# A Hymba layer on one core: other banks in the output projection, token sums kept in DRAM, buffers laid out anew

## The chip, the core and the metric

The kernel runs on one core of a Trainium2 chip. TensorE (PE in the profile) multiplies matrices into PSUM banks, VectorE (DVE) and ScalarE (ACT) work element by element, GpSimd (POOL) and SyncE (SP) issue the transfers between DRAM and the core's on-chip memory. The metric is the time of one execution in microseconds on the device, the median of several runs: before the change 2355.78 us (2355.51 to 2356.0, three runs).

## The reference

One layer on 2048 tokens of width 1024: a mixing part (retention and short convolution, one output projection) and a gated feed-forward part of width 2816, each behind a modulated norm.

```python
        h = modulate(rms_norm(x, norm1_g[layer]), shift1, scale1)
        proj = h @ w_in[layer]
        # rotary, retention_chunkwise, group norm, gate: y_ret; short convolution: y_conv
        mixed = jnp.concatenate([y_ret, y_conv], axis=-1) @ w_out[layer]
        x = x + gate1[:, None, :] * mixed

        h = modulate(rms_norm(x, norm2_g[layer]), shift2, scale2)
        up = h @ w_up[layer]
        a, val = up[..., :D_FF], up[..., D_FF:]
        a = causal_dwconv(a, ffn_conv_w[layer]) + ffn_conv_b[layer]
        ffn = (jax.nn.silu(a) * val) @ w_down[layer]
        x = x + gate2[:, None, :] * ffn
    fmod = (c_act @ final_mod_w + final_mod_b).reshape(b, 2, d)
    return modulate(rms_norm(x, final_norm_g), fmod[:, 0], fmod[:, 1])
```

## The kernel before

Everything is fp32. Each operand of a product is split in two parts, hi (a cast, on ACT: L214 for activations, L777 and L91 for weights) and lo (the difference, on DVE: L215, L778, L92), and `mm3` makes three matmuls of each product: hi by hi (L233), hi by lo (L234), lo by hi (L235). So a matmul waits for ACT where it is the first with an operand, and for DVE where it is the first with that operand's lo part.

The work has three stages with two changes between them and a third in the middle of the second stage.

**Mixing**, four blocks b of 512 tokens. Each ends with `out_proj(b)`: two halves `mg` of four blocks of 128 output rows, each half with four weight tiles and in the same four banks, tagged "mm". DVE evicts a bank at L489 (`xr`), POOL stores it to `x1d`, and the sum of squares is made up. `between` runs other work after each weight tile: in block 3 that is `Tokens.chunk`, which makes the inputs of the up stage. After block 3 stands `norm2(3)`: two matmuls (L178) into the bank "misc", a reciprocal root on ACT and DVE, and a store to `r2d`.

**Up**, two halves B of 1024 tokens with 22 units each (`Up`). A unit computes gate and value columns of two blocks with seven products instead of eight, from seven sums of tokens (11, 21, T2, T1, T3, T4, 22) and four sums of weights (`Weights`: a, s, b, c). A product is 12 matmuls of 512 columns, a unit 84. `start` does 11 and 21, `middle` T2, T1, T3, `finish` T4 and 22, and the `finish` of a unit stands after the `start` of the next. ACT copies partial sums out of the banks (`snap`, L817), the gated results go to DRAM (`gd`) by POOL (L858, L862). The token sums of the second half are made at `i == FC`, in the place where the first half ends: loads from `x1d` (L699), modulation (L700, L701), four differences, seven splits, for each of four chunks.

**Down**, five blocks of columns (three of 512, two of 256), 22 steps k each. A step loads a weight tile (L89, 512 KB) and a tile of `gd` (L986), splits both, and adds to seven banks, the eighth lagging by three steps. At a block's end DVE evicts the banks at L928 with the residual, which SP loads (L927, `acc`).

A tile scheduler sets the order of the instructions on every engine from the code and the buffers. Each engine then runs its instructions in that order, and so do the DMA queues of SP and POOL. Pools are opened and closed at the stage changes; a new pool's buffers lie where closed ones lay and wait for their last readers.

## Time and profile before

| | us |
|---|---|
| median of three runs | 2355.78 |
| the profiled execution | 2353.7 |
| its span | 2351.6 |
| PE busy | 2261.1 |
| DVE busy | 1651.2 |
| ACT busy | 1033.2 |

The mean granted clock of TensorE was 0.984 of full speed. "Busy" PE includes time at the lower clock; an idle time in brackets is the time in which an engine waited just before the instruction, with the instruction that ended it. The windows give busy time by engine, with the number of instructions, the granted clock (PEclk; 1.00 is 2.4 GHz, 0.50 is 1.2 GHz), the share of the DMA engines' time and what they moved.

### The profile page before, as it was taken

How to read it: one execution, taken by the hardware profiler on the slowest of the kernel's cores; microseconds unless marked ns; L12 is line 12 of the kernel's file. 1: busy time of each engine (PE TensorE's matmuls, PEld its weight loads, DVE VectorE, ACT ScalarE, POOL GpSimd, SP SyncE). 2: the span in 40 equal slices, each digit the busy share in tenths (PEclk: the TensorE clock that was granted, in tenths of full speed). 3: DMA queues.
4: the chain of work that ended last, by engine and by line, in shares of the span. 5: the costliest groups of instructions: out<-in, count | busy, mean ns of one | idle time of the engine just before them, and what ended most of it. 6: DMA issues, size and time to landing. Idle time of an engine off the chain costs nothing.

```text
span 2351.6 us, 29468 instructions
## 1 busy us (share of the span) xinstructions
PE 2261.1 (96%) x10838; PEld 1881.4 (80%) x10838; DVE 1651.2 (70%) x3033; ACT 1033.2 (44%) x1536; POOL 87.9 (4%) x171
## 2 busy tenths in 40 slices
PE   8999999999999998699999989999999799999997
PEld 5888788878888887588888867888888688888897
DVE  8999659875986699866666688666665336363765
ACT  5255325532553346544444455444443225252564
POOL 0000000000000000000000000000000000000000
PEclk9999999999999999899999989999999899999999
DMA  8443734463355324322222242222221645454574
GB/s 308 152 135 115 248 94 131 136 227 113 112 169 202 117 90 144 121 87 84 81 83 89 84 134 81 82 81 81 81 86 52 248 148 195 155 188 159 173 249 156
DMA packets 121505, 321.44 MB, mean 137 GB/s; under 512 B 14656, under 2 KB 23376, under 8 KB 121360
## 3 DMA queue, kind: packets, MB, share of 16 engines
q1 hardware_dynamic: 108864, 279.30, 36.7%
q0 software_dynamic: 12352, 40.13, 4.3%
q8 instruction: 85, 1.39, 0.2%
q14 instruction: 60, 0.49, 0.1%
q10 hardware_dynamic: 144, 0.13, 0.0%
HBM read 278.60 MB, written 40.89 MB: 136 GB/s over the span
## 4 chain that ended last, share of the span: by engine, by line
issue 65%; PE 23%; DVE 5%; POOL 3%; DMA 2%; ACT 1%; SPq 0%; POOLq 0%; DVEq 0%; ACTq 0%
PE mm L235 4%; PE mm L234 4%; PE mm L233 4%; PE sc L235 2%; PE sc L234 2%; PE sc L233 2%; POOL g L858 1%; DMA x<-in_x 1%; POOL g L862 1%; PE y L235 1%; PE y L234 1%; PE y L233 1%; DVE w L92 1%; PE misc L233 1%; PE misc L235 1%
## 5 line engine op out<-in xcount | busy, mean ns | idle before, releaser
L92 DVE TENSOR_TENSOR w<-raw,w 128x1024 fp32r<-128x1024 f32 x249 | 303.6, 1221 | 328.0 <-ACT w L91 327.6
L91 ACT CAST w<-raw 128x1024 fp32r<-128x1024 f32 x249 | 261.4, 1050 | 478.3 <-PE misc L235 208.8
L233 PE MATMUL mm<-act,w 128*128 128x512 f32 x816 | 324.2, 398 | 10.7 <-ACT act L214 5.5
L234 PE MATMUL mm<-act,w 128*128 128x512 f32 x816 | 319.7, 392 | 0.1
L235 PE MATMUL mm<-act,w 128*128 128x512 f32 x816 | 318.4, 392 | 0.8 <-DVE w L92 0.8
L233 PE MATMUL sc<-act,w 128*128 128x512 f32 x528 | 207.0, 393 | 13.7 <-ACT w L777 8.5
L777 ACT CAST w<-raw 128x1024 fp32r<-128x1024 f32 (+1 forms) x176 | 143.0, 836 | 151.6 <-PE mm L235 81.8
L234 PE MATMUL sc<-act,w 128*128 128x512 f32 x528 | 207.2, 392 | 1.3 <-DVE act L215 1.2
L235 PE MATMUL sc<-act,w 128*128 128x512 f32 x528 | 207.0, 392 | 0.0
L778 DVE TENSOR_TENSOR w<-raw,w 128x1024 fp32r<-128x1024 f32 (+1 forms) x176 | 167.3, 956 | 41.6 <-ACT w L777 41.5
L233 PE MATMUL mm<-w,act 128*128 128x512 f32 x480 | 187.8, 393 | 8.1 <-DVE xr L489 4.4
L233 PEld LDWEIGHTS mm<-act,w 128*128 128x128 f32 x816 | 154.5, 189 | 43.3 <-DVE xr L489 6.3
L234 PE MATMUL mm<-w,act 128*128 128x512 f32 x480 | 187.4, 390 | 0.0
L235 PE MATMUL mm<-w,act 128*128 128x512 f32 x480 | 186.6, 391 | 0.0
L235 PEld LDWEIGHTS mm<-act,w 128*128 128x128 f32 x816 | 154.0, 189 | 34.3 <-DVE w L92 1.5
L234 PEld LDWEIGHTS mm<-act,w 128*128 128x128 f32 x816 | 154.4, 189 | 31.8 <-DVE act L215 1.0
L233 PE MATMUL mm<-g,w 128*128 128x512 f32 (+1 forms) x440 | 150.8, 350 | 15.3 <-ACT g L214 14.9
L234 PE MATMUL mm<-g,w 128*128 128x512 f32 (+1 forms) x440 | 153.2, 350 | 1.4 <-DVE g L215 1.2
L235 PE MATMUL mm<-g,w 128*128 128x512 f32 (+1 forms) x440 | 153.0, 349 | 0.8 <-DVE w L92 0.8
L233 PEld LDWEIGHTS sc<-act,w 128*128 128x128 f32 x528 | 99.5, 189 | 37.3 <-ACT w L777 9.0
L823 DVE TENSOR_TENSOR a<-sn,mm 128x512 f32<-128x512 f32 x44 | 30.3, 688 | 141.0 <-PE mm L235 140.9
L234 PEld LDWEIGHTS sc<-act,w 128*128 128x128 f32 x528 | 99.9, 189 | 23.4 <-DVE act L215 2.9
(282 smaller groups left out, 4670.9 us busy)
## 6 DMA issues: line engine op xcount, KB each, us to landing
raw<-in_w_down SPq DMA_DIRECT2D x110, 512.0 KB, 4.2
raw<-in_w_up SPq DMA_DIRECT2D x88, 512.0 KB, 3.5
raw<-in_w_tok SPq DMA_DIRECT2D x64, 512.0 KB, 5.0
x<-in_mod_w SPq DMA_DIRECT2D x96, 256.0 KB, 4.1
raw<-in_w_conv SPq DMA_DIRECT2D x48, 512.0 KB, 3.6
gr<-g SPq DMA_DIRECT2D x66, 256.0 KB, 3.7
raw<-in_w_out SPq DMA_DIRECT2D x32, 512.0 KB, 3.5
x<-in_x SPq DMA_DIRECT2D x56, 256.0 KB, 4.2
```

Source lines behind the costliest of these rows:

```text
L91: S.copy(w[:, 0, :], raw)
L92: V.tensor_tensor(w[:, 1, :], raw, w[:, 0, :].bitcast(F32), op=ALU.subtract)
L233: T.matmul(out, lhs[0], rhs[0], start=first, stop=False, skip_group_check=on)
L234: T.matmul(out, lhs[0], rhs[1], start=False, stop=False, skip_group_check=on)
L235: T.matmul(out, lhs[1], rhs[0], start=False, stop=last, skip_group_check=on)
L777: S.copy(w[:, 0, cs], src)
L778: V.tensor_tensor(w[:, 1, cs], src, w[:, 0, cs].bitcast(F32), op=ALU.subtract)
L823: V.tensor_tensor(at[:, 2 + o : 514 + o], part, ps, op=ALU.add)
L858: nc.gpsimd.dma_start(gd[2 * B][j], self.sl0)
L862: nc.gpsimd.dma_start(gd[2 * B + 1][j], sl1)
```

## The change

1. In `out_proj`, the second half accumulates into the banks "sc0", "sc1", "y" and "misc"; the first half keeps "mm". This holds for all four blocks.
2. The weights of the first up unit are loaded and split inside `out_proj(3)`, after its weight tiles 4, 6 and 7 (`last`), from the weight pools of the mixing stage, which stay open through the up stage (4 split buffers and 3 raw ones in place of 5 and 4). The first unit takes four "mm" banks. `norm2(3)` moves behind the `middle` of unit 0.
3. `Ahead` makes the second half's token sums in 16 steps, called at units 1 to 16, in five buffers `xa` and one buffer `xs`; each of the 28 sums is stored to DRAM by POOL (512 KB, `Ahead.put`), and 28 loads on SP (`fetch`) bring them back: three T3 into new buffers, the others into the buffers of the first half's sums as these come free. The in-place work at `i == FC` is gone. The new weights' `one` stands after the `finish` of the unit before.
4. In the down stage the pools are opened in another order (raw tiles, `gr`, split weights first, `acc` later), so that they lie elsewhere. With `END = 4`, the last four steps of each bank but the eighth are done together.

The core of the diff (the modulation, the differences and the splits of `Ahead.step` are those of `Tokens.chunk`, four parts per chunk):

```diff
-            ps = [ps_mm() for _ in range(4)]
+            ps = [ps_tag(t) for t in (("mm",) * 4, ("sc0", "sc1", "y", "misc"))[mg]]
...
-    act2 = p2.enter_context(tc.tile_pool(name="act2", bufs=12, reuse_waits="tile"))
+    act2 = p2.enter_context(tc.tile_pool(name="act2", bufs=4, reuse_waits="tile"))
...
+    class Ahead:
...
+        def tmp(self):
+            return self.pool.tile([128, 512], F32, tag="xa", bufs=5, name=nm("xa"))
+        def put(self, n, i, u):
+            t = split_into(self.pool.tile([128, 2, 512], F32R, tag="xs", bufs=1, name=nm("xs")), u)
+            nc.gpsimd.dma_start(xd[n][i], t.bitcast(F32))
+        def step(self, q):
+            i, part = divmod(q, 4)
+            if part == 0:
+                r = load_r2(b, self.tmp())
+                self.h11 = h2_f32(b, i, r, self.tmp())
+                self.put("11", i, self.h11)
...
+    def fetch(n, i, t):
+        nc.sync.dma_start(t.bitcast(F32), xd[n][i])
+        return t
...
-    norm2(3, ss2)
-    p3.close()
-    pf.close()
-    wts.close()
...
-    whlp = p4.enter_context(tc.tile_pool(name="whlp2", bufs=5, side="right", reuse_waits="tile"))
-    rawp = p4.enter_context(tc.tile_pool(name="rawp2", bufs=4, side="right", reuse_waits="tile"))
+    ss2 = out_proj(3, mixed, spread(cv[3].norm, lambda k: tk.chunk(k) if k < 4 else None,
+                                    {4: nxt.raw, 6: nxt.one, 7: nxt.two}))
+    for i in range(4):
+        tk.late(i)
+    nxt.three()
...
+            self.tags = ("mm", "mm") if B == 0 and j == 0 else (("sc0", "y"), ("sc1", "misc"))[j % 2]
...
         if i == FC:
             last.finish()
             last = None
-            tk = Tokens(2, [load_r2(2, new_ss()), load_r2(3, new_ss())], tmp)
             for c in range(4):
-                tk.chunk(c)
+                for n in ("T4", "22"):
+                    X2[n].append(fetch(n, c, x_slot(n)))
+            X = X2
...
         u.start()
         if more:
             nxt.raw()
-            nxt.one()
+        if i == FC - 1:
+            for c in range(4):
+                for n in ("11", "21"):
+                    X2[n].append(fetch(n, c, x_slot(n)))
         if last is not None:
             last.finish()
         if more:
+            nxt.one()
             nxt.two()
         u.middle()
+        if i == 0:
+            norm2(3, ss2, "mm")
...
+        if 1 <= i <= 16:
+            ahead_x.step(i - 1)
+        if i == FC - 2:
+            t3 = [fetch("T3", c, act3.tile(...)) for c in range(3)]
+        if i == FC - 1:
+            for n in ("T2", "T1"):
+                X2[n] += [fetch(n, c, x_slot(n)) for c in range(4)]
+            X2["T3"] = t3 + [fetch("T3", 3, x_slot("T3"))]
...
-    whlp, gp, rawp, grp = pool("whlp3", 6), pool("gp", 6), pool("rawp3", 3), pool("grp", 4)
-    accp, fo, sp = pool("accp", 18), pool("fo2", 4), pool("sp2", 8)
+    rawp, grp, whlp, fo = pool("rawp3", 3), pool("grp", 4), pool("whlp3", 6), pool("fo2", 4)
+    gp, accp, sp = pool("gp", 6), pool("accp", 18), pool("sp2", 8)
...
             for m in range(KC - 1):
-                part(m, k)
+                for kk in (k,) if k < FC - END else range(FC - END, FC) if k == FC - 1 else ():
+                    part(m, kk)
```

What this does to the order of the engines is shown at three places.

The first place is the end of `out_proj(3)` on PE. Before (`misc_8408` is the bank of `norm2(3)`, `w_8447` the weights a of up unit 0):

```order
L233 MATMUL mm_8230<-act_6798,w_8270 128x512
L234 MATMUL mm_8230<-act_6798,w_8270 128x512
L235 MATMUL mm_8230<-act_6798,w_8270 128x512
L178 MATMUL misc_8408<-q_8405,onesr 128x512 x2
L233 MATMUL sc_8468<-act_8007,w_8447 128x512
L234 MATMUL sc_8468<-act_8007,w_8447 128x512
L233 MATMUL mm_8484<-act_8014,w_8447 128x512
L235 MATMUL sc_8468<-act_8007,w_8447 128x512
```

With the change (`w_8353` is the same weight a):

```order
L233 MATMUL misc_8258<-act_6798,w_8302 128x512
L234 MATMUL misc_8258<-act_6798,w_8302 128x512
L235 MATMUL misc_8258<-act_6798,w_8302 128x512
L233 MATMUL mm_8466<-act_8035,w_8353 128x512
L234 MATMUL mm_8466<-act_8035,w_8353 128x512
L233 MATMUL mm_8482<-act_8042,w_8353 128x512
L234 MATMUL mm_8482<-act_8042,w_8353 128x512
L235 MATMUL mm_8466<-act_8035,w_8353 128x512
```

The two matmuls of `norm2(3)` no longer stand between the projection and unit 0 (they are found inside unit 1), and the projection's last matmuls go to "y" and "misc". On DVE, 82 rows lie between the first eviction of `out_proj(3)` and the lo part of unit 1's weight a. On PE the first matmul that needs that lo part stands 62 rows behind the first of unit 0, which follows the 96 matmuls of the projection's second half.

The second place is the middle of the up stage on SP's queue. Before (`raw` is a weight of an up unit, `x_2_0` and the like the tokens of the second half, `r` their norm):

```order
L770 DMA raw_11324<-in_w_up 128x1024
L771 DMA raw_11325<-in_w_up 128x1024
L770 DMA raw_11667<-in_w_up 128x1024
L771 DMA raw_11668<-in_w_up 128x1024
L741 DMA ss_11458<-r_2_129 128x512
L699 DMA fo_11462<-x_2_0_111 128x512
L699 DMA fo_11476<-x_3_0_119 128x512
L770 DMA raw_11768<-in_w_up 128x1024
L741 DMA ss_11460<-r_3_130 128x512
L699 DMA h_11469<-x_2_4_115 128x512
```

With the change, in the same place, the loads of sums 11 and 21 begin behind the weights of unit 22:

```order
L801 DMA raw_11560<-in_w_up 128x1024
L802 DMA raw_11561<-in_w_up 128x1024
L783 DMA act_11564<-x_0_7906 128x1024
L783 DMA act_11566<-x_0_7910 128x1024
L783 DMA act_11568<-x_1_7907 128x1024
```

and further on, the last sums (T4, 22) are followed by the weights of unit 23:

```order
L783 DMA act_11738<-x_2_7932 128x1024
L783 DMA act_11740<-xT_3_7929 128x1024
L783 DMA act_11742<-x_3_7933 128x1024
L801 DMA raw_11781<-in_w_up 128x1024
L802 DMA raw_11782<-in_w_up 128x1024
```

The token loads, which DVE and ACT had to work on, have become loads of finished sums, and the weights of unit 23 stand behind 25 of them. Each of these 25 waits for PE's last reading of the buffer it fills. The other three (T3) stand between the weights of units 12 and 13.

The third place is the beginning of the down stage on SP's queue. Before, the last of 17 residual loads, and then the first weights and gated tiles:

```order
L927 DMA acc_16254<-x_1_6_109 128x512
L927 DMA acc_16272<-x_1_7_110 128x512
L927 DMA acc_17048<-x_2_0_111 128x512
L89 DMA raw_14630<-in_w_down 128x1024
L986 DMA gr_14635<-g_0_7818 128x512
L89 DMA raw_14668<-in_w_down 128x1024
```

With the change (the first row is the last weight of the up stage):

```order
L802 DMA raw_14467<-in_w_up 128x1024
L89 DMA raw_14745<-in_w_down 128x1024
L1043 DMA gr_14750<-g_0_7818 128x512
L89 DMA raw_14783<-in_w_down 128x1024
L1043 DMA gr_14788<-g_1_7819 128x512
L89 DMA raw_14814<-in_w_down 128x1024
L1043 DMA gr_14819<-g_2_7820 128x512
L1043 DMA gr_14850<-g_3_7821 128x512
L984 DMA acc_15417<-x_0_0_95 128x512
```

Three weight tiles and four gated tiles now stand ahead of the residual loads. The first weight and the first gated tile wait for PE's last reading of the buffers under them, sums T4 and 22.

## Rows read from the trace of the kernel before

**Rows 1.** The page, part 1: each engine's busy time.

```profile
PE 2261.1 (96%) x10838; PEld 1881.4 (80%) x10838; DVE 1651.2 (70%) x3033; ACT 1033.2 (44%) x1536; POOL 87.9 (4%) x171
```

**Rows 2.** Windows: us, busy (xcount) of PE PEld DVE ACT POOL, PEclk, DMA share, GB/s.

```profile
915.00:970.00 55.00, 28.76 (x102) 20.81 (x101) 52.44 (x83) 33.26 (x54) 3.77 (x7) 0.78 0.42 143
1385.00:1425.00 40.00, 26.67 (x78) 16.89 (x78) 38.26 (x62) 29.32 (x49) 0.54 (x1) 0.79 0.38 118
1820.00:1850.00 30.00, 14.99 (x54) 11.72 (x54) 11.17 (x15) 8.66 (x12) 1.08 (x2) 0.72 0.84 301
1000.00:1350.00 350.00, 350.00 (x1546) 289.82 (x1545) 235.33 (x365) 150.78 (x220) 19.97 (x37) 1.00 0.25 84
```

**Rows 3.** PE's waits, grouped: total, times, longest.

```profile
PE mm L233 <- ACT g L214: 14.9, 2, 14.3
PE misc L178 <- ACT q L214: 9.7, 1, 9.7
PE mm L233 <- DVE xr L489: 9.5, 5, 2.6
PE mm L233 <- ACT act L214: 9.0, 3, 5.5
```

**Rows 4.** Timeline, PE, at the first change (start, us, instruction, [idle before]).

```profile
918.61 0.50 PE L233 MATMUL mm<-act,w 128*128 128x512 f32 x1 [2.59 <-DVE xr L489]
949.85 0.80 PE L178 MATMUL misc<-q,onesr 128*128 128x512 f32 x1 [9.74 <-ACT q L214]
961.95 0.79 PE L233 MATMUL sc<-act,w 128*128 128x512 f32 x1 [8.51 <-ACT w L777]
```

**Rows 5.** Timeline, DVE and SP, at the first change.

```profile
906.78 0.74 DVE L489 SCALAR_TENSOR_TENSOR xr<-mm,mod,xr 128x512 f32<-128x512 f32 x1
...
953.55 0.33 SPq L770 DMA_DIRECT2D raw<-in_w_up  x1
```

**Rows 6.** Windows of 5 us: the second change, the down stage, the third change.

```profile
1415.00:1420.00 5.00, 2.69 (x10) 1.35 (x8) 5.00 (x10) 4.70 (x8) 0.00 (x0) 1.00 0.19 52
1855.00:1860.00 5.00, 5.00 (x24) 4.14 (x23) 0.00 (x0) 0.00 (x0) 0.00 (x0) 1.00 0.98 356
1825.00:1830.00 5.00, 1.59 (x8) 0.97 (x6) 2.50 (x5) 0.98 (x2) 0.44 (x1) 0.93 0.99 352
```

**Rows 7.** DMA issues from 1000 to 1350: KB each, median us to landing.

```profile
raw<-in_w_up SPq DMA_DIRECT2D x37, 512.0 KB, 3.5
g<-ss POOLq DMA_DIRECT2D x19, 256.0 KB, 2.8
```

**Rows 8.** Timeline at the third change: PE, ACT, SP.

```profile
1840.93 1.65 PE L233 MATMUL mm<-g,w 128*128 128x512 f32 x3 [14.34 <-ACT g L214]
...
1829.83 0.63 ACT L830 ACTIVATE cv<-cv 128x512 f32<-128x512 f32 x1 [1.61 <-DVE cv L827]
1837.84 1.04 ACT L91 CAST w<-raw 128x1024 fp32r<-128x1024 f32 x1 [7.38 <-DMA raw<-in_w_down]
...
1820.21 10.79 SPq L927 DMA_DIRECT2D acc<-x  x17
1831.25 0.33 SPq L89 DMA_DIRECT2D raw<-in_w_down  x1
```

**Rows 9.** Groups by line and form, 1000 to 1350: busy, mean ns, idle before.

```profile
L777 ACT CAST w<-raw 128x1024 fp32r<-128x1024 f32 x37 | 39.0, 1054 | 55.4 <-PE mm L235 39.5 <-PE y L235 8.1 <-PE misc L235 7.8
L778 DVE TENSOR_TENSOR w<-raw,w 128x1024 fp32r<-128x1024 f32 x37 | 45.3, 1225 | 20.0 <-ACT w L777 20.0
L817 ACT COPY sn<-sc 128x512 f32<-128x512 f32 x37 | 21.7, 587 | 60.6 <-PE sc L235 60.6
L777 ACT CAST w<-raw 128x512 fp32r<-128x512 f32 x36 | 20.6, 619 | 9.7 <-PE misc L235 4.9 <-PE y L235 4.8
```

**Rows 10.** Timeline, PE: block ends of the down stage.

```profile
2207.60 0.39 PE L234 MATMUL mm<-g,w 128*128 128x256 f32 x1 [0.45 <-DVE g L215]
...
2291.18 0.39 PE L233 MATMUL mm<-g,w 128*128 128x256 f32 x1 [0.59 <-ACT g L214]
```

More of the change, by code (lines that the diff above doesn't have):

```diff
@@ L602, in hybrid_layer, with spread @@
     ss2 = None
-    def spread(norm, chunk):
+    def spread(norm, chunk, last=None):
         cut = ((), (0, 1), (2, 3), (4,), (5,), (6,), (7,), ())
         return [lambda i=i: (norm() if i == 0 else None, [chunk(k) for k in cut[i]],
-                             more_mod() if i in (4, 5) and mod_left else None) for i in range(8)]
+                             more_mod() if i in (4, 5) and mod_left else None,
+                             last[i]() if last and i in last else None) for i in range(8)]
     for b in range(NB):
@@ L689, in hybrid_layer, with x_slot @@
     gd = [[dram.tile([128, 512], F32, tag=f"g_{b}_{j}", name=f"g_{b}_{j}") for j in range(FC)] for b in range(NB)]
-    def new_x2():
-        return act2.tile([128, 2, 512], F32R, tag="act2", name=nm("act"))
+    NAMES = ("11", "21", "T2", "T1", "T3", "T4", "22")
+    xd = {n: [dram.tile([128, 2, 512], F32, tag=f"x{n}_{i}", name=f"x{n}_{i}") for i in range(4)] for n in NAMES}
+    def x_slot(n):
+        if n[0] == "T" and n != "T4":
+            return act2.tile([128, 2, 512], F32R, tag=n, name=nm("act"))
+        return new_act()
     def split_into(dst, u):
@@ L745, in new_hx @@
         return hx.tile([128, 512], F32, tag=tag, bufs=bufs, name=nm("hx"))
-    tk = Tokens(0, [load_r2(0, new_hx("r", 2)), load_r2(1, new_hx("r", 2))], ft, lambda: new_hx("t4", 4))
-    ss2 = out_proj(3, mixed, spread(cv[3].norm, lambda k: tk.chunk(k) if k < 4 else None))
-    assert not mod_left
-    for i in range(4):
-        tk.late(i)
-    norm2(3, ss2)
-    p3.close()
-    pf.close()
-    wts.close()
-    p4 = ExitStack()
-    ap_ = p4.enter_context(tc.tile_pool(name="ap_", bufs=2, reuse_waits="tile"))
-    p4.enter_context(tc.tile_pool(name="sp3", bufs=7, side="right")).tile([128, 8], F32, tag="s", name="sp3")
-    whlp = p4.enter_context(tc.tile_pool(name="whlp2", bufs=5, side="right", reuse_waits="tile"))
-    rawp = p4.enter_context(tc.tile_pool(name="rawp2", bufs=4, side="right", reuse_waits="tile"))
     class Weights:
@@ L803, in three @@
             self.split(self.c, slice(0, 512), self.wv[:, 0:512])
+    nxt = Weights(0)
+    tk = Tokens(0, [load_r2(0, new_hx("r", 2)), load_r2(1, new_hx("r", 2))])
+    ss2 = out_proj(3, mixed, spread(cv[3].norm, lambda k: tk.chunk(k) if k < 4 else None,
+                                    {4: nxt.raw, 6: nxt.one, 7: nxt.two}))
+    assert not mod_left
+    for i in range(4):
+        tk.late(i)
+    nxt.three()
+    p3.close()
+    pf.close()
+    p4 = ExitStack()
+    ap_ = p4.enter_context(tc.tile_pool(name="ap_", bufs=2, reuse_waits="tile"))
+    pa_ = ExitStack()
+    ahead_x = Ahead(2, pa_.enter_context(tc.tile_pool(name="xa", bufs=1, side="right", reuse_waits="tile")))
     def product(ps, w, c0, x, first):
@@ L862, in finish @@
             nc.gpsimd.dma_start(gd[2 * B + 1][j], sl1)
-    nxt = Weights(0)
-    nxt.raw()
-    nxt.one()
-    nxt.two()
-    nxt.three()
-    last = None
+    last, X, X2 = None, tk.X, None
     for i in range(2 * FC):
@@ L891, in hybrid_layer @@
             nxt.raw()
-            nxt.one()
+        if i == FC - 1:
+            X2 = {n: [] for n in NAMES}
+            for c in range(4):
+                for n in ("11", "21"):
+                    X2[n].append(fetch(n, c, x_slot(n)))
         if last is not None:
@@ L900, in hybrid_layer @@
         last = u
+        if 1 <= i <= 16:
+            ahead_x.step(i - 1)
+        if i == 17:
+            pa_.close()
+            act3 = pa_.enter_context(tc.tile_pool(name="act3", bufs=3, side="right", reuse_waits="tile"))
+        if i == FC - 2:
+            t3 = [fetch("T3", c, act3.tile([128, 2, 512], F32R, tag="T3", name=nm("act"))) for c in range(3)]
+        if i == FC - 1:
+            for n in ("T2", "T1"):
+                X2[n] += [fetch(n, c, x_slot(n)) for c in range(4)]
+            X2["T3"] = t3 + [fetch("T3", 3, x_slot("T3"))]
     last.finish()
+    pa_.close()
     p4.close()
+    wts.close()
     p2.close()
```

76 lines of the change are left out of this document (45 added, 31 removed).

## The prediction

> **What bounds the kernel now.** First the busy times [rows 1]: PE works 2261.1 us of a span of 2351.6, DVE 1651.2, so a gain has to come out of the time in which PE waits or runs slowly. Then the windows [rows 2]. In the steady up stage PE is busy for 350.00 of 350 us at clock 1.00, with 1546 matmuls, 0.2264 us each, so a unit of 84 takes 19.02 us and nothing can be gained there. In the windows of the three changes of stage the same price explains only a part: 102 matmuls are worth 23.1 us of the first one's 55, 78 are worth 17.7 of the second's 40, 54 are worth 12.2 of the third's 30. So 31.9, 22.3 and 17.8 us are lost, 72.0 together, in idle time and at a granted clock of 0.78, 0.79 and 0.72. Then PE's waits [rows 3] and the timelines [rows 4, 5, 8] say what ends each loss.
>
> **First change: out_proj(3) to unit 0.** Before, the projection's second half waits for DVE's evictions of the first (2.59 us, and 2.57 once more), then PE waits 9.74 us for the norm's sum of squares and 8.51 for the first up weight [rows 4], whose load is issued only at 953.55 [rows 5]. With the change the second half has banks of its own, the norm's matmuls stand inside unit 1, and weight a of unit 0 is split inside the projection. What is late next is DVE. It was busy for 52.44 of 55 us in 83 instructions [rows 2], 0.632 each, and its order still has 82 rows between its first eviction, at 906.78 [rows 5], and the lo part of unit 1's weight a. Those take 51.8 us; with 1.8 us of DVE's own waiting (an estimate from the 2.6 us that it was idle in that window) and 1.22 for the lo part itself [rows 9] it is ready at 961.6. PE, without a wait, would start the second half at 918.61 - 2.59 = 916.02 and want that part 96 + 62 matmuls later, at 951.8. So PE loses 9.8 us up to there, in several waits for lo parts. I add 2 us for weights and the norm's matmuls behind it, and 2 for a clock that drops in the longest wait: 14 us lost instead of 31.9, a gain of 17.9. Bounds: if DVE's idle time is worth nothing and the waits are too short for the clock, 8 us are lost; if DVE stays as far behind as before and only the two waits of 9.74 and 8.51 go halfway, 21. So a gain of 11 to 24.
>
> **Second change: unit 21 to unit 22.** Before, the sums are made in place and DVE is busy for 5.00 of 5 us [rows 6]. With the change this is 25 loads of 512 KB on one queue, each behind PE's last reading of its buffer. The down stage shows what such transfers get: 356 GB/s at a DMA share of 0.98 [rows 6], so 1.47 us each. In matmul time a product takes 2.72 us. The nine loads for T2, T1 and the fourth T3 take 13.2 us from the moment when PE has read T2 in unit 21, and the eight for T4 and 22 follow them, 25.0 us in all; PE gets to T4 of unit 22 after two products of unit 21's middle, two of its finish and five of unit 22, 24.5 us. Behind these come the two weights of unit 23 (2.9 us for the pair, 1.05 for the cast, 1.22 for the difference [rows 9]), needed two products later at 29.9 and ready at 30.2. On this count the queue and PE run level; every store of g that shares the time puts PE behind. I take 5 us lost, between 0 (all of it hidden) and 12 (eight of the loads, 11.8 us, uncovered), instead of 22.3: a gain of 17.3, from 10 to 22.
>
> In a sentence apart, since the rate decides here: the Trainium skill (DMA: Bandwidth & Descriptors, section Bandwidth) derives 436 GB/s for the DMA fabric, and its Specifications put the memory's side at about 358. By the first an estimate for each load is 1.20 us, the 25 loads take 6.7 us less, the loss is 0 and the sum 2303; the trace agrees with the second, 356 [rows 6].
>
> **Third change: up to down.** Before, 17 residual loads occupy SP from 1820.21 to 1831.0, the first weight is issued at 1831.25, its cast is at 1837.84, and PE waits 14.34 us for g until 1840.93 [rows 8]. With the change three weights and four g tiles stand ahead of the residuals, in buffers which PE has read two products before its end. Then ACT is late next: the last gate's silu ends at 1829.83 + 0.63 = 1830.46, then come a weight cast, 1.05, and a g cast, 0.62 [rows 9], so PE starts at about 1832.2. Gain 8.7 us. The idle time of 5.6 us is still long enough for the clock to fall (it was 0.93 in the 5 us in which this wait began [rows 6]), so I give nothing for a faster start. Bounds: 6 if the first g tile lands 2.7 us late, 11 if the clock stays up for half of the first matmuls.
>
> **Smaller terms.** The three earlier blocks lose their waits for evictions: 9.5 us in five [rows 3] less 2.59 and 2.57 leaves 4.3. In the down stage five waits at the block ends, 2.92 us in sum, the first of 0.45 and the last of 0.59 [rows 10], may go; against that PE comes to step 21 some 14 us of matmuls earlier (63 of them), and a weight may land late. Between a loss of 4 (one load of 3.5 us [rows 7] uncovered) and a gain of 2.9 I take 0.6.
>
> **What the steps of Ahead cost.** ACT and DVE get work in up units: 28 splits, 16 modulations, 16 differences, some 60 DVE instructions and 44 on ACT, 38 and 27 us by the prices above, beside PE in units where DVE is busy for 0.67 of the time and ACT for 0.43 [rows 2]. That cover is enough, but the single buffer `xs` chains the 28 sums: the cast of the next waits for the store of the last, and the snapshot that frees PE's bank stands behind it on ACT. A store of 256 KB lands in 2.8 us [rows 7]; 512 KB are bounded by 2.8 and 5.6. With a cast (0.62) and a difference (0.69) a sum takes 4.1 to 6.9 us; the order puts two or three into a unit of 19.02. ACT waits 60.6 us before 37 snapshots [rows 9], 1.6 each, so small delays vanish there. I take a loss of 1.5 us, between 0 and 10 (0.36 for each sum).
>
> **The sum.** 17.9 + 17.3 + 8.7 + 4.3 + 0.6 - 1.5 = 47.3 us. From the profiled execution's 2353.7 that leaves 2306.4; the median of the runs is 2.1 above that execution, so 2308.5, and I say 2308. The terms' bounds, taken as independent, give about 11 us to either side: 2297 to 2319.
>
> **Rivals.**
>
> *The queue of loads is late* (0.18). If each of the 25 fetches also shares its time with stores and weights, the middle costs 15 us or more, and waits of that size lower the clock, as to 0.72 to 0.79 in the windows of before [rows 2]. With the first change at the bad end, 19 lost, the gain falls by 10 + 5: 2323. For it speaks that queue and PE run level in my count; against it, a DMA share of only 0.25 outside [rows 2].
>
> *Everything is covered* (0.10). The good ends together: 6 us more than forecast at the first change, 5 at the second, 2.3 at the third, 1.5 for Ahead, 14.8 in all: 2294. For it speaks that ACT and SP have room in every window of [rows 2]; against it, that DVE has none at the first change.
>
> *The chain through xs decides* (0.06, slower). One mechanism: a store of 512 KB lands so late that the next cast holds ACT, the snapshots behind it come late, and PE waits for its bank. 28 sums have 11 units of 19.02 us by the order, 7.5 us each. To cancel the gain each must cost PE 47.3 / 28 = 1.7 us, which is so once a store takes 7.5 + 1.7 - 1.3 = 7.9 us, nearly three times the 2.8 of half the size. At 9.5 us it costs 3.3 each, 92 in sum: about 2400. Against it speaks that stores now land in 2.8 us while DVE is busy for two thirds of the time. The Trainium skill (SBUF — State Buffer, section on its two separate sides) warns of just this: a DMA issued by POOL can wait for its descriptors while DVE holds a port that the two share. Here DVE and POOL stores have shared the whole up stage and the 2.8 us do not show it.
>
> *The change does not do what it says* (0.04). Buffers freed too late would put the weights of unit 0 and the first loads of the down stage back where they were; then mainly the 4.3 us of the earlier blocks remain against Ahead's cost, 2352, within 0.2%.
>
> **How the numbers follow.** The forecast has 0.62. Its range with the late queue and half of what lies beyond is 2292 to 2330. Differences under 0.2%, 4.7 us, cannot be told from no change. Faster: 0.62 + 0.18 + 0.10 and a little of the last two, 0.91; no change 0.03; slower 0.06.
>
> **What the profile of the changed kernel would show.** First change: PE's waits on POOL's or ACT's norm are gone, waits on DVE lo parts add up to about 10 us between the projection and unit 1. Second: no idle over 5 us, DMA at about 350 GB/s for some 35 us. Third: PE begins the down stage 5 to 6 us after the last up matmul, released by ACT's cast of g, residual loads behind it. Steady units with Ahead: 19.0 us, PE never waiting for a snapshot. I am wrong if units 1 to 11 are longer than 19.4 us, if the weights of unit 23 end a long wait, or if the first g waits for a DMA.

## The result, and the profile after

| | before | after |
|---|---|---|
| median of four runs, us | 2355.89 | 2323.68 (2322.29 to 2325.16) |
| ratio to before, 95% interval | | 0.9858 (0.9841 to 0.9876) |
| the profiled execution, us | 2353.7 | 2324.19 |
| its span, us | 2351.6 | 2322.3 |
| mean granted clock | 0.984 | 0.991 |

The change makes the kernel 32 us faster, where 48 were forecast. The page's first part, which answers to [rows 1], shows PE busy for 8.5 us less with as many matmuls, at a higher mean clock, and 28 more instructions on POOL, the stores of the sums:

```profile
PE 2252.6 (97%) x10838; PEld 1877.5 (81%) x10838; DVE 1667.5 (72%) x3033; ACT 1029.6 (44%) x1536; POOL 102.9 (4%) x199
```

POOL's first store to `gd` in each unit is a milestone that stands at the same place of the program in both traces. With these, the first matmul of the last projection's second half (909.33 before, 908.84 after), the first matmul of the down stage (1840.93, 1808.33) and the matmul that broadcasts the last norm (2341.26, 2309.72), the gain can be laid out by stretch. Each number is the difference of the two times at a milestone, less that at the milestone before; they add up to the difference of the two profiled spans, 29.3 us, where the medians differ by 32.2:

| stretch | forecast | measured |
|---|---|---|
| three earlier blocks | 4.3 | 0.5 |
| last projection to the end of unit 0's first result | 17.9 | 13.3 |
| units 1 to 11 (Ahead) | -1.5 | -6.5 |
| units 21 to 25 (second change) | 17.3 | 21.3 |
| last up matmul to first down matmul | 8.7 | 4.1 |
| down stage | 0.6 | -1.1 |
| from the last norm's matmul to the end | 0 | -2.2 |
| sum of the spans' difference | 47.3 | 29.3 |

Windows of the changed kernel, with the columns of [rows 2]. The first three cover the three changes of stage, the fourth the units with Ahead, the fifth units without it:

```profile
908.00:965.00 57.00, 42.05 (x172) 32.98 (x171) 53.95 (x86) 38.56 (x60) 3.78 (x7) 0.94 0.50 168
1355.00:1395.00 40.00, 39.33 (x173) 32.09 (x172) 19.83 (x31) 13.25 (x19) 2.70 (x5) 1.00 0.94 372
1795.00:1825.00 30.00, 19.75 (x75) 15.82 (x74) 14.75 (x19) 10.53 (x14) 1.08 (x2) 0.77 0.75 264
975.00:1165.00 190.00, 184.35 (x810) 151.38 (x809) 164.79 (x262) 105.96 (x165) 25.77 (x48) 1.00 0.54 191
1200.00:1350.00 150.00, 150.00 (x663) 124.23 (x662) 105.94 (x160) 64.86 (x95) 8.63 (x16) 1.00 0.23 83
```

In 190 us with Ahead PE made 810 matmuls, which are 183.4 us at 0.2264; in the 150 us without it 663, which are all of them. The second change is nearly a steady stretch now, with 173 matmuls in 40 us.

PE's waits, which answer to [rows 3]:

```profile
PE mm L233 <- ACT g L214: 10.2, 1, 10.2
PE sc L235 <- DVE w L92: 8.3, 2, 7.9
PE sc L233 <- ACT fo L864: 5.6, 4, 1.9
PE mm L235 <- DVE q L809: 3.5, 1, 3.5
PE mm L233 <- DVE v L319: 1.6, 3, 0.8
```

The waits for evictions (L489) and the 9.7 us for the norm (misc L178 on q) are gone. In their place stand waits for lo parts, for snapshots (L864) and for the retention's v, and the wait for g is 10.2 in place of 14.3.

**First change.** PE's timeline, which answers to [rows 4]; "sc" is the first bank of the projection's second half, and the row at 908.84 its first matmul:

```profile
908.84 0.39 PE L233 MATMUL sc<-act,w 128*128 128x512 f32 x1
929.61 1.22 PE L235 MATMUL sc<-act,w 128*128 128x512 f32 x2 [7.91 <-DVE w L92]
944.69 0.50 PE L235 MATMUL mm<-act,w 128*128 128x512 f32 x1 [2.15 <-DVE w L809]
959.35 0.50 PE L235 MATMUL mm<-act,q 128*128 128x512 f32 x1 [3.49 <-DVE q L809]
962.90 0.50 PE L235 MATMUL sc<-act,w 128*128 128x512 f32 x1 [0.98 <-DVE w L809]
```

The second half begins at 908.84, without a gap. Its third weight is cast by ACT in time, but DVE begins the lo part only at 928.34, behind 34 rows, most of them token work (first fence ACT, second DVE):

```profile
904.20 1.05 ACT L91 CAST w<-raw 128x1024 fp32r<-128x1024 f32 x1
```

```profile
928.34 1.22 DVE L92 TENSOR_TENSOR w<-raw,w 128x1024 fp32r<-128x1024 f32 x1
```

The matmul at 962.90 waits for the lo part of unit 1's weight a, for which the prediction had 961.6.

**Second change.** Two of the 5 us windows over the fetches, with the columns of [rows 6], and the two waits of PE that are left there:

```profile
1360.00:1365.00 5.00, 5.00 (x24) 4.14 (x23) 4.21 (x7) 2.44 (x4) 0.54 (x1) 1.00 1.02 416
1385.00:1390.00 5.00, 4.50 (x20) 3.38 (x19) 0.00 (x0) 0.68 (x2) 0.00 (x0) 1.00 1.03 420
```

```profile
1390.18 0.50 PE L233 MATMUL sc<-act,w 128*128 128x512 f32 x1 [0.68 <-ACT sn L864]
1397.84 0.51 PE L235 MATMUL sc<-act,w 128*128 128x512 f32 x1 [1.01 <-DVE w L809]
```

With the fetches, and POOL's stores of g among them, the DMA engines move 416 and 420 GB/s at a share of 1.02 and 1.03, not 356; PE waits 1.7 us in all.

**Units with Ahead.** One of four such places. PE waits for the snapshot `fo`; on ACT, ahead of it, the cast into `xs` waited for the store of the sum before, and DVE waited for that cast and was late with the gate's L874, for which ACT's next instruction waits (PE, then ACT, then DVE):

```profile
1000.76 0.50 PE L233 MATMUL sc<-act,q 128*128 128x512 f32 x1 [1.71 <-ACT fo L864]
```

```profile
995.84 0.62 ACT L214 CAST xs<-xa 128x512 fp32r<-128x512 f32 x1 [1.98 <-DMA x<-xs]
997.88 0.63 ACT L877 ACTIVATE ss<-ss 128x512 f32<-128x512 f32 x1 [1.42 <-DVE ss L874]
1000.13 0.57 ACT L864 COPY fo<-sc 128x512 f32<-128x512 f32 x1
```

```profile
996.49 0.69 DVE L215 TENSOR_TENSOR xs<-xa,xs 128x512 fp32r<-128x512 f32 x1 [1.25 <-ACT xs L214]
997.10 0.74 DVE L874 SCALAR_TENSOR_TENSOR ss<-a,cp,ss 128x512 f32<-128x512 f32 x1
```

**Third change.** PE, ACT and POOL, which answer to [rows 8]. ACT's weight cast is done at 1802.9, but its g cast stands until 1807.66:

```profile
1808.33 1.65 PE L233 MATMUL mm<-g,w 128*128 128x512 f32 x3 [10.25 <-ACT g L214]
...
1801.85 1.03 ACT L91 CAST w<-raw 128x1024 fp32r<-128x1024 f32 x1
1807.66 0.62 ACT L214 CAST g<-gr 128x512 fp32r<-128x512 f32 x1 [4.78 <-issue]
...
1802.97 0.54 POOL L909 DMA_DIRECT2D g<-cv  x1 [6.05 <-DVE zeros L1026]
```

The g tile was loaded in time. In ACT's order the cast waits also for POOL's queue: the new buffer `g` lies over the up stage's last gate result, and the store of that, issued at 1802.97, lands 4.6 us later, at 1807.6.

**The end.** After the last transfer has landed (2316.9) POOL still runs a DRAIN, with which the program closes. POOL's DRAINs in the kernel before, in the changed one and in the run with the sums stored in halves, below (minimum, median and maximum in ns):

```profile
L1086 POOLq DRAIN  x3: 45/102/4959, 2345.8 to 2351.3; - x3
L1145 POOLq DRAIN  x3: 45/102/7246, 2314.3 to 2322.1; - x3
L1149 POOLq DRAIN  x3: 45/93/9534, 2326.6 to 2336.7; - x3
```

The long one takes 4.96, 7.25 and 9.53 us; POOL had issued 159, 187 and 215 transfers. So each set of 28 more stores adds 2.3 us here, 0.08 us for each.

### The profile page after: what moved, and what is told of

It is laid out like the page before. It is cut to its first block, busy times and chain, and to the rows that moved or that the text cites. A ratio compares the mean times of both kernels' runs of the same rounds, so it can differ in the third digit from the quotient of the medians.

```text
span 2322.3 us, 29557 instructions
## 1 busy us (share of the span) xinstructions
PE 2252.6 (97%) x10838; PEld 1877.5 (81%) x10838; DVE 1667.5 (72%) x3033; ACT 1029.6 (44%) x1536; POOL 102.9 (4%) x199
## 3 DMA queue, kind: packets, MB, share of 16 engines
q1 hardware_dynamic: 113760, 295.55, 38.7%
## 4 chain that ended last, share of the span: by engine, by line
issue 79%; PE 7%; DVE 7%; POOL 4%; DMA 3%; ACT 1%; POOLq 0%; SPq 0%; DVEq 0%; ACTq 0%
PE mm L233 2%; PE mm L234 2%; PE mm L235 2%; POOL g L909 1%; DMA x<-in_x 1%; POOL g L905 1%; DVE mw L162 1%; DVE w L92 1%; POOL x L490 1%; DMA x<-in_mod_w 0%; POOL out L1014 0%; DVE rope L283 0%; PE sc L235 0%; PE sc L234 0%; PE sc L233 0%
## 5 line engine op out<-in xcount | busy, mean ns | idle before, releaser
L233 PE MATMUL mm<-act,w 128*128 128x512 f32 x708 | 280.2, 396 | 0.0
L235 PE MATMUL mm<-act,w 128*128 128x512 f32 x708 | 276.7, 391 | 2.1 <-DVE w L809 2.1
L234 PE MATMUL mm<-act,w 128*128 128x512 f32 x708 | 276.5, 391 | 0.0
L235 PE MATMUL sc<-act,w 128*128 128x512 f32 x580 | 227.0, 392 | 10.3 <-DVE w L92 8.3
L233 PE MATMUL sc<-act,w 128*128 128x512 f32 x580 | 226.3, 390 | 1.4 <-ACT sn L864 1.4
L234 PE MATMUL sc<-act,w 128*128 128x512 f32 x580 | 226.2, 390 | 0.0
L808 ACT CAST w<-raw 128x512 fp32r<-128x512 f32 (+1 forms) x176 | 142.3, 834 | 127.5 <-PE mm L235 64.8
L809 DVE TENSOR_TENSOR w<-raw,w 128x512 fp32r<-128x512 f32 (+1 forms) x176 | 164.1, 954 | 44.9 <-ACT w L808 44.8
L233 PE MATMUL mm<-g,w 128*128 128x512 f32 (+1 forms) x440 | 151.4, 350 | 12.2 <-ACT g L214 10.2
L235 PEld LDWEIGHTS mm<-act,w 128*128 128x128 f32 x708 | 133.2, 188 | 31.0 <-DVE w L809 2.6
L234 PEld LDWEIGHTS mm<-act,w 128*128 128x128 f32 x708 | 133.6, 189 | 26.7
L233 PEld LDWEIGHTS mm<-act,w 128*128 128x128 f32 x708 | 133.4, 188 | 26.6
L235 PEld LDWEIGHTS sc<-act,w 128*128 128x128 f32 x580 | 109.3, 189 | 34.6 <-DVE w L92 9.2
L233 PEld LDWEIGHTS sc<-act,w 128*128 128x128 f32 x580 | 109.1, 188 | 25.0 <-ACT sn L864 2.4
L234 PEld LDWEIGHTS sc<-act,w 128*128 128x128 f32 x580 | 109.2, 188 | 22.6
```

The costliest lines, as they stand in the source:

```text
L233: T.matmul(out, lhs[0], rhs[0], start=first, stop=False, skip_group_check=on)
L234: T.matmul(out, lhs[0], rhs[1], start=False, stop=False, skip_group_check=on)
L235: T.matmul(out, lhs[1], rhs[0], start=False, stop=last, skip_group_check=on)
L808: S.copy(w[:, 0, cs], src)
L809: V.tensor_tensor(w[:, 1, cs], src, w[:, 0, cs].bitcast(F32), op=ALU.subtract)
```

## The experiments

All were timed in five rounds beside the kernel before; ratios are to it. Times of different sets are compared by these ratios, since the kernel before itself had medians of 2356.8 to 2357.8 in them. No kernel with part 2, 3 or 4 alone was run: what each of these gave is read from the stretches of the trace.

### Part 1 alone

```diff
 (kernel before)
-            ps = [ps_mm() for _ in range(4)]
+            ps = [ps_tag(t) for t in (("mm",) * 4, ("sc0", "sc1", "y", "misc"))[mg]]
```

> The kernel before with part 1 alone: the second half of every output projection in sc0, sc1, y, misc. The term of the prediction (the waits for evictions simply go) asks for 4.3 us less in the three earlier blocks and up to 5.2 more in the last one: 2346 to 2351. The theory from the trace of the changed kernel says that DVE, not the bank, is what PE waits for there: the waits on the evictions come back as waits on other DVE results (v, act), and in the last block the norm's sums end no earlier, so 0 to 1.5 us less: 2354 to 2356.

Measured: 2352.91 us beside 2356.77, ratio 0.9985 (0.9975 to 0.9995), so 1 to 6 us less; the profiled span, 2351.9, shows none of it. By the clock alone the two expectations are not told apart. The trace tells how the waits moved:

```profile
275.04 0.47 PE L233 MATMUL mm<-w,act 128*128 128x512 f32 x1 [1.76 <-DVE v L319]
...
930.46 1.22 PE L235 MATMUL sc<-act,w 128*128 128x512 f32 x2 [8.10 <-DVE w L92]
950.70 0.79 PE L178 MATMUL misc<-q,onesr 128*128 128x512 f32 x1 [9.09 <-ACT q L214]
```

The waits for L489 are gone in every block. In the next block, PE now waits for v (three times, 1.76, 0.62 and 0.64, 3.0 in all, where it waited 4.4 for evictions), and in the last block it waits 8.10 for the lo part of a weight and then 9.09 for the norm, at 950.70 (9.74 at 949.85 before). So the wait went from the bank to DVE, and in the profiled execution the mixing stage hardly gained: PE's waits up to the last projection's second half are 18.3 us in place of 19.3. What makes the median 1 to 6 us less is not shown.

### The sums stored in halves

```diff
-            t = split_into(self.pool.tile([128, 2, 512], F32R, tag="xs", bufs=1, name=nm("xs")), u)
-            nc.gpsimd.dma_start(xd[n][i], t.bitcast(F32))
+            hi = self.pool.tile([128, 512], F32R, tag="xh", bufs=1, name=nm("xh"))
+            lo = self.pool.tile([128, 512], F32R, tag="xl", bufs=1, name=nm("xl"))
+            S.copy(hi, u)
+            nc.gpsimd.dma_start(xd[n][i][:, 0, :], hi.bitcast(F32))
+            V.tensor_tensor(lo, u, hi.bitcast(F32), op=ALU.subtract)
+            nc.gpsimd.dma_start(xd[n][i][:, 1, :], lo.bitcast(F32))
```

> The changed kernel, each token sum stored in two halves from two buffers of half the size (the same 4 KB in all): the hi half is stored while the lo half is made, so the next cast waits for 256 KB and not for 512. If the landing of the 512 KB store (3.8 to 5.1 us) in the chain through xs is what makes units 2 to 10 longer, their four waits before snapshots (5.6 us) mostly go: 4 to 6.5 us less, 2317 to 2320. The rival, that the added work on ACT and DVE or the smaller weight pools lengthen these units, expects no change, 2323, or a little more for 28 more transfers.

Measured: 2339.54 us, ratio 0.9931 (0.9919 to 0.9943), 16 to 17 us slower than the changed kernel. The expectation fell. PE's waits before snapshots were 14.9 us, in seven units one after the other, and the DRAIN at the end is 2.3 us longer. The first and the last store of a hi half were issued 159.8 us apart, against 169.7 for the whole sums in the changed kernel: the scheduler had packed the sums closer still. That a shorter link does not help if the chain is then packed more densely is the reading; it is not shown here, since the edit also doubles POOL's stores of sums and changes the order on ACT.

### Ahead tied to its units

```diff
+        def pace(self, u):
+            t = self.tmp()
+            V.tensor_copy(t[:, 0:2], u.at[:, 0:2])
+            return t
...
-                r = load_r2(b, self.tmp())
+                r = load_r2(b, self.pace(u))
...
-                r = load_r2(b + 1, self.tmp())
+                r = load_r2(b + 1, self.pace(u))
```

> The changed kernel once more, unaltered, on the chip of the runs beside it, so that they have a comparison there: 0.9858 of the kernel before, 2321 to 2326 us, with four or five waits before snapshots in units 2 to 10 and 10 us before the first matmul of the down stage.

> The changed kernel, the loads of Ahead tied to the unit beside which they stand (a small copy from that unit's buffer a is written into the tile that is loaded), so that the 28 sums stretch over some 13 units where they stood in 9.5. If their density on the in-order queues of ACT and DVE is what makes snapshots late, the waits before snapshots fall from 5.7 us (6 to 9 in the runs on this chip) to under 2.5: 3 to 6 us less than the unaltered one. The rival, that each of the 28 sums costs its own wait for the store of the last one, expects the same 5.7 us, spread over more units: no change.

Measured: the unaltered kernel 2325.05, ratio 0.9865 (0.9851 to 0.9878), with four waits before snapshots, 5.4 us. The paced one 2318.17, ratio 0.984 (0.9826 to 0.9853), 6.9 us less, with waits of 0.82 and 0.31; by the milestones units 1 to 11 are 6.5 us shorter. The stores of the sums in the changed kernel (first fence) and in the paced one (second): who waited for them, us and times, and their landing.

```profile
  ACT xs L214: 44.6, 23
DMA to landing us min/median/max: 2.8/3.8/5.1
```

```profile
  ACT xs L214: 17.1, 13
DMA to landing us min/median/max: 2.8/2.9/4.6
```

The same 28 sums, now 250 us from the first store to the last, 9.3 apart in place of 6.3: ACT's waits for the store fall from 44.6 us to 17.1. So it is the density on the in-order queues, and not the number of sums, that makes the snapshots late.

### gp opened before fo2

```diff
-    rawp, grp, whlp, fo = pool("rawp3", 3), pool("grp", 4), pool("whlp3", 6), pool("fo2", 4)
-    gp, accp, sp = pool("gp", 6), pool("accp", 18), pool("sp2", 8)
+    rawp, grp, whlp, gp = pool("rawp3", 3), pool("grp", 4), pool("whlp3", 6), pool("gp", 6)
+    fo, accp, sp = pool("fo2", 4), pool("accp", 18), pool("sp2", 8)
```

> The changed kernel, pool gp opened before fo2 in the down stage, so that the first g tile no longer lies over the buffer of the last gate result, whose store is issued at 1802.97 and lands 4.6 us later. If that store is what ends the 10.25 us wait, PE starts the down stage 4 to 5 us earlier, after ACT's casts: 2318.5 to 2320. The rival, that the loads (DMA share 0.98 there) or the second weight would be late in any case, expects 0 to 1.5 us.

Measured: 2320.64 us, ratio 0.9851 (0.9835 to 0.9867). The interval holds the changed kernel's ratio, so the clock alone does not settle it. PE's first matmul of the down stage does:

```profile
1806.50 1.65 PE L233 MATMUL mm<-g,w 128*128 128x512 f32 x3 [5.38 <-ACT g L214]
```

The wait is 5.38 us, where the prediction had counted 5.6 for it. In the three other runs with this edit, below, it is 5.38 too, and 10.1 to 11.3 in all runs without it.

### END = 1

```diff
-    LAG, END = 3, 4
+    LAG, END = 3, 1
```

> The changed kernel with END = 1, the banks of the down stage ended step by step as before. By the two traces the down stage from its first matmul to the last column sum is 1.05 us longer with END = 4 (496.5 to 497.6 for the last big matmuls, waits of 1.99 and 0.76 on a weight at the fourth block): 1 us less, 2322 to 2323. The prediction's term expects 0.6 us more; if END hides evictions at all five block ends, 2 to 3 more.

Measured: 2328.95 us, ratio 0.9881 (0.9869 to 0.9894), 4 to 5 us slower, against the trace, whose down stage was 498.4 us from its first matmul to the last norm's, the shortest of all. What was longer was the up stage, where nothing is changed, not even the order: units 1 to 11 took 5.7 us more than in the changed kernel's trace, with waits before snapshots of 8.8 us in place of 5.6. The same comparison without these waits stands below.

### The first change: lo parts left out, and made by POOL

The first kernel leaves the lo parts of T1, T2 and T3 of the first half out of the sums; the products read the hi part in their place.

```diff
         def put(self, n, u):
-            self.X[n].append(split_into(x_slot(n), u))
+            x = x_slot(n)
+            S.copy(x[:, 0, :], u)
+            if n in ("T1", "T2", "T3"):
+                x = Hi(x)          # x[:, q, :] gives the hi part for both q
+            else:
+                V.tensor_tensor(x[:, 1, :], u, x[:, 0, :].bitcast(F32), op=ALU.subtract)
+            self.X[n].append(x)
```

> The changed kernel without the lo parts of the sums T1, T2 and T3 of the first half, which leaves those out of the result: the products read the hi part twice. Twelve DVE instructions of 0.60 us less inside the last output projection, everything else the same. If DVE is the bound of the first change, the waits on DVE between the projection and unit 1 (15.0 us) fall by about 7 us and the time by as much, 2315 to 2318. The rival, that the place of single lo parts in DVE's order or the late loads set these waits, expects at most 2 us.

Measured: 2322.15 us, ratio 0.9854 (0.984 to 0.9867), 2.9 us less than the unaltered kernel beside it, with intervals that overlap; in the trace the first unit's result is 1.7 us earlier. PE's waits there are 11.5 us in place of 12.7 to 15.0, and what ends them has changed:

```profile
929.09 0.50 PE L233 MATMUL sc<-act,w 128*128 128x512 f32 x1 [3.19 <-ACT w L91]
949.08 0.80 PE L233 MATMUL sc<-act,w 128*128 128x512 f32 x1 [4.62 <-ACT w L821]
957.63 0.54 PE L233 MATMUL mm<-act,q 128*128 128x512 f32 x1 [2.18 <-ACT fo L877]
```

With 7 us of DVE's work gone, PE waits for casts of weights and for a snapshot, on ACT. So DVE is the first of two bounds that lie close together, and "7 us" was too much.

The second kernel makes the same twelve lo parts on POOL:

```diff
-            self.put("T2", t2)
-            self.put("T1", h11)
+            self.put("T2", t2, nc.gpsimd)
+            self.put("T1", h11, nc.gpsimd)
...
-            self.put("T3", h12)
+            self.put("T3", h12, nc.gpsimd)
```

> The changed kernel with the same twelve lo parts made by POOL in place of DVE, nothing left out. If POOL works beside DVE without disturbing it, this saves what leaving them out saves, 5 to 7 us. The Trainium skill (SBUF — State Buffer, section on its two separate sides) says that POOL and a DVE instruction with two inputs from this memory lock each other out of a shared port; by that DVE waits as long as POOL works, and the time is that of the changed kernel or worse, 2323 to 2330, with longer DVE instructions beside POOL's in the trace.

Measured: 2335.72 us, ratio 0.9908 (0.9895 to 0.9922), 10.7 us slower, beyond what was expected. Groups of DVE instructions from 905 to 960, with busy time and mean ns, in this kernel (first) and in the changed one (second):

```profile
L92 DVE TENSOR_TENSOR w<-raw,w 128x1024 fp32r<-128x1024 f32 x2 | 4.6, 2300 | 0.0
```

```profile
L92 DVE TENSOR_TENSOR w<-raw,w 128x1024 fp32r<-128x1024 f32 x2 | 2.4, 1216 | 0.0
```

and a row of POOL's timeline in this kernel:

```profile
932.76 5.56 POOL L720 TENSOR_TENSOR act<-fi,act 128x512 fp32r<-128x512 f32 x3 [7.26 <-ACT act L719]
```

The 1024-wide lo parts went from 1216 to 2300 ns, the sums of squares (L211) from 682 to 1218 on average. POOL takes 1.3 to 2.3 us for a lo part, once 4.5, for which DVE took 0.68. Nine DVE instructions with two inputs from on-chip memory are some 1.1 us longer beside POOL, 9.6 in sum, more than the 7.2 (twelve of 0.60) that were taken from DVE; the evictions at L489, which read a bank, keep their 0.74. So the trace agrees with what the Trainium skill (SBUF — State Buffer, section on its two separate sides) states.

Most of the 10.7 us is another thing. PE's longest wait in this place, and what ACT waited for ahead of it:

```profile
961.79 0.79 PE L233 MATMUL mm<-act,w 128*128 128x512 f32 x1 [10.86 <-ACT sn L867]
```

```profile
961.15 0.59 ACT L867 COPY sn<-mm 128x512 f32<-128x512 f32 x1 [6.23 <-DMA x<-xr]
```

The snapshot's buffer was free only when the store of an eviction had landed. DVE had evicted that bank by 949.63, but POOL was at its lo parts until 953.05 and issued the store in between, at 952.99; it landed at 961.01. In the changed kernel POOL issued it at 946.19, it landed at 948.44, and PE did not wait. So arithmetic on POOL delays the stores that stand behind it in POOL's order. Why the landing took 8.0 us in place of 2.3 was not examined.

### Both mends, with END = 4 and END = 1, and the token work spread

The kernels are the pacing and the order of `gp` together; then with `END = 1`; then, in place of that, with

```diff
-        cut = ((), (0, 1), (2, 3), (4,), (5,), (6,), (7,), ())
+        cut = ((), (0, 1), (2, 3), (4,), (5,), (6,), (7,), ()) if last is None else ((), (0,), (1,), (), (2,), (3,), (), ())
```

> The changed kernel with both mends, Ahead tied to its units and gp opened before fo2. If the two losses are separate, their gains add: 6.9 us (2325.05 to 2318.17 on one chip) and 2.7 to 4.9 us (2323.3 to 2320.6 by the clock, 10.25 to 5.38 us in the trace's wait): 2312 to 2316. If pacing and the down stage's start have something in common, such as the traffic of the stores, 2317 to 2318.

> The same with END = 1. The run with END = 1 alone was 5 us slower by the clock, though its down stage, from the first matmul to the last column sums, was the shortest of all (498.4 us, 499.7 to 502.0 in four others): its up stage, with the very same order, had 8.8 us of waits before snapshots in place of 5.7. If those waits were chance, they are gone with the pacing, and END = 1 is 1 to 3 us faster than the run beside it. If END = 4 is truly worth something, 4 to 5 us slower.

> The kernel with both mends, the four chunks of token work in the last output projection spread over its weight tiles 1, 2, 4 and 5 in place of two each at 1 and 2. In DVE's order the lo part of the second half's third weight, for which PE waits 7.9 us, then stands 8 rows earlier, some 5 us. If the place in DVE's order sets this loss, 2 to 5 us less than the run beside it; if the sum of the work on DVE, ACT and the loads does, the wait comes back at the weights of units 0 and 1: within 1 us.

| kernel | us | ratio, 95% interval | first down matmul to last norm |
|---|---|---|---|
| pace, gp | 2316.23 | 0.9826 (0.9813 to 0.9839) | 502.3 |
| pace, gp, END = 1 | 2311.80 | 0.9808 (0.9795 to 0.9822) | 498.9 |
| pace, gp, cut | 2314.25 | 0.982 (0.9807 to 0.9833) | 501.1 |

The two mends add up to the upper end of what was expected. With `END = 1` the down stage is 3.3 us shorter and the kernel 4.4 us faster than the one beside it (the intervals overlap, the trace agrees): END = 4 costs time. The place is in the middle of the fourth block, some 30 us after its first matmul (2161.92 and 2158.31). Windows of 10 us there, with END = 4 (first) and END = 1 (second; us, PE busy (x), PEclk, DMA share, GB/s), and PE's two waits in the first:

```profile
2190.00:2200.00 10.00, 7.54 (x49) 0.83 0.90 296
```

```profile
2188.00:2198.00 10.00, 9.24 (x75) 1.00 0.89 298
```

```profile
2193.29 0.39 PE L233 MATMUL mm<-g,w 128*128 128x256 f32 x1 [1.71 <-ACT w L91]
2194.55 0.39 PE L235 MATMUL mm<-g,w 128*128 128x256 f32 x1 [0.75 <-DVE w L92]
```

With END = 4 PE comes to this step while its weight is still on the way: its load, issued at 2184.64 behind residual loads that waited for ACT's output of the third block, landed at 2192.17. PE waits 1.71 us for ACT's cast and 0.75 for the lo part, and the granted clock falls to 0.83: 49 matmuls in 10 us, where 75 are made with END = 1, with a wait of 0.76 there.

The kernel with END = 1 is the fastest of all, 46 us below the one before. The spread of the token work is 2.0 us faster, within the intervals; PE's waits show that the wait came back:

```profile
923.30 0.73 PE L235 MATMUL sc<-act,w 128*128 128x512 f32 x2 [2.86 <-DVE w L92]
945.06 0.80 PE L233 MATMUL mm<-act,w 128*128 128x512 f32 x1 [2.92 <-ACT w L813]
959.87 0.80 PE L233 MATMUL mm<-act,q 128*128 128x512 f32 x1 [4.00 <-ACT fo L869]
```

2.86 us in place of 7.65 for the third weight, and then 2.92 for a weight of the up stage and 4.00 for a snapshot; all waits of PE in this place are 12.3 us, against 14.2 in the kernel beside it.

## Why the prediction was right in its sign and too large

**Right.** The order of things: the three changes of stage held the loss, and they gave 38.7 us; all other stretches together gave 9 of it back. The second change went better than forecast and the slower rival did not come about: stores of 512 KB land in 3.8 us, 5.1 at most, within the bounds that were given.

**Luck.** The measured 2323.7 lies beyond the 2297 to 2319 of the terms' bounds. It is the number of the rival with the late queue, 2323, but not its mechanism: that has 15 us or more lost at the second change, where PE waited 1.7.

**Its own signs.** Of the three signs of being wrong two came true. Units 1 to 11 took 215.9 us, 19.63 each, where 19.4 was the limit. The first g did wait for a DMA, POOL's store, and PE began the down stage 10.6 us after the last up matmul and not 5 to 6. The weights of unit 23 end a wait of 1.01 us, not a long one.

**First change, 13.3 in place of 17.9.** The step that failed is "PE, without a wait, would start the second half at 918.61 - 2.59 = 916.02". DVE's side was right to 1.3 us (962.90 for 961.6). But before, too, PE had gone on into the second half, in the two banks that were evicted first, and did 28 of its matmuls before it first waited, at 916.02. This is its first one there in the kernel before:

```profile
909.33 0.39 PE L233 MATMUL mm<-act,w 128*128 128x512 f32 x1
```

Counted from 908.84, PE wants unit 1's lo part at 944.6, and 17 us are lost up to there, not 9.8; the waits add up to 15.0. Before, those 28 matmuls were work done ahead of the first wait, and I counted them once more. With the 4 us that the sum adds behind it, the gain would have been 10.9 and not 13.3: most of these 4 did not come, the granted clock was 0.94 over the window. That DVE alone was the bound is half right: with 7 us less on DVE, ACT's casts come next.

**Earlier blocks, 0.5 in place of 4.3.** The failed step is "the three earlier blocks lose their waits". The bank was free, but PE then came to the next product of DVE that much earlier: 1.6 us of waits for v and 0.6 for P (L382) stand there now, and the waits on DVE at L434 stayed (5.1, 5.5 before). Only part of a removed wait is a gain where the same engine is behind what follows: from 100 us on, PE's waits up to 909 fell from 9.8 to 7.2 us. The rest of the difference is chance: in the first 100 us, where nothing is changed, PE waited 11.6 us in place of 9.4, and between 8.5 and 11.7 over all runs.

**Ahead, -6.5 in place of -1.5.** The mechanism was named, as the slower rival, and its size was off in the sum. The term that was mis-sized is the time between sums: I had 7.5 us from 11 units, the trace has 6.3, since the scheduler drew the steps forward until the chain through `xs` was nearly full: 3.8 for the landing, 0.54 for the issue, 0.62 and 0.69 for the split, 5.7 us in sum. The run with pacing shows that this density was the cause.

**Second change, 21.3 in place of 17.3.** The count itself held: PE was at T4 of unit 22 24.7 us after it had read T2 of unit 21 (at 1389.50 and 1364.76; 24.5 counted), and the 25 loads landed 1.47 us apart on the average (from 1356.48 to 1391.74). But these 1.47 us hold four stores of g as well: where no store shared the time, loads landed 1.2 to 1.3 us apart. The mis-sized term is the 5 us on top of the count, for which "every store of g that shares the time puts PE behind" was the reason; PE waited 1.7, of which 0.68 were for a snapshot. In the sentence on the Trainium skill I took the trace's side against the larger rate; for the loads alone the other end of its two figures, 436, was nearer (1.26 us each by 416 GB/s, 1.20 by 436): the loss is 1.7 us, where that rule gave 0. This rests on the trace; no run tested it.

**Third change, 4.1 in place of 8.7.** The failed step is "then ACT is late next". The weight and the first g tile came in time, but the buffer for the split g was not free until 1807.6. The count had the places of raw tiles, `gr` and weights in it, and not that of `gp`. With `gp` elsewhere the step holds: PE waits 5.38 us, where it gave 5.6.

**Down stage, -1.1 in place of 0.6.** END = 4 was taken at a gain of 0.6 and costs 3.3 in the pair of runs that differ in nothing else. The five waits, 2.92 us in sum, on which the gain rested were misread: none stands at a block's end [rows 10] and none is for an eviction. The first comes 4 us after the fourth block's first matmul (2203.64), the next three 23 to 35 us after it, the last more than 20 us into the fifth block; they are for g and for weights. The step "a weight may land late" came true in the fourth block, and the clock, which the term had left out, made more of it: of the 34 matmuls of 0.12 us that are missing in those 10 us, the waits explain some 20, and the granted clock of 0.83 the rest.

**The end, -2.2 in place of 0.** The term was put at nothing without a reason. The 28 new stores make POOL's DRAIN at the end of the program longer, 7.25 us in place of 4.96, after all of them have landed. It is 4.96 with part 1 alone and 7.25 in all ten traces with POOL's 28 stores, so it follows the number of transfers that POOL has issued; why it does is not shown.

## What to carry to other kernels

A wait that is removed is worth only the distance to what ends next on the same engine: list, for each, everything the waiting instruction needs, the buffer it writes into as well, and who last read it. Work that is moved off the critical place and given to in-order engines needs a pace: here the scheduler packed it until its own chain was nearly full and the engines' urgent work stood behind it. Look also at what an engine issues: arithmetic on POOL held up POOL's stores. Before a loss is priced by the matmuls in a window, look whether work from the window had been done ahead of it.

## What the runs showed of the hardware

- DMA: with 25 loads of 512 KB on SP's queue, read from DRAM that the kernel itself had written, and four stores of g among them, the DMA engines moved 382 to 420 GB/s in the six windows of 5 us from 1360 to 1390, at a share of 1.02 to 1.03; weights and `gr` in the down stage had moved 356 at 0.98 [rows 6]. The 358 GB/s of the memory's side that the Trainium skill (DMA: Bandwidth & Descriptors, section Specifications) states was exceeded here.
- A store issued by POOL beside a DVE that was busy for 0.87 of the time (164.79 of 190 us) landed in 3.8 us for 512 KB, and in 2.9 where the stores stood further apart. Stores with no other transfer beside them landed in 2.9 also while DVE was busy throughout (those issued at 997.48, 1011.59 and 1132.22): no sign of the descriptor wait of which the Trainium skill (SBUF — State Buffer, section on its two separate sides) warns. POOL's own arithmetic did stop DVE's instructions with two inputs from on-chip memory, as the same section says, and not those that read a bank (0.74 us beside it).
- POOL's DRAIN at the end of the program took 4.96, 7.25 and 9.53 us with 159, 187 and 215 transfers issued by POOL, 0.08 us more for each, though all had landed before it ended.
- The same up stage, in the same order, had 5.4 to 8.8 us of waits before snapshots in five traces. That a nearly full chain makes chance in the landing of transfers visible in the time is my reading of it; with pacing the waits were 0 to 1.5 us in four traces.
